# A second group of FFN tiles in plain products, and the first convolution tap on ACT, in a four-layer encoder

## The chip, the cores and the metric

The kernel runs on one core of a Trainium2 chip. The metric is device microseconds of one execution. The engines are PE (TensorE: matmuls; PEld is its weight load), DVE (VectorE), ACT (ScalarE), POOL (GpSimd) and SP (which issues most DMAs).

## The reference

An encoder of four layers over T = 528 tokens (16 meta tokens and 512 of the sequence) with 1024 features. Each layer has a mixer (MLA, RWKV-7, RG-LRU, MLA in turn), a layer norm, a feed-forward part (FFN) and a layer norm. The change lies in the FFN alone:

```python
def _conv_glu_ffn(x, w_in, conv_w, conv_b, w_out):
    g, u = jnp.split(x @ w_in, 2, axis=-1)
    g = _dw_conv(g, conv_w, conv_b, FFN_CONV_LEFT)
    return (jax.nn.silu(g) * u) @ w_out
...
f = _conv_glu_ffn(h, ffn_w_in[i], ffn_conv_w[i], ffn_conv_b[i], ffn_w_out[i])
h = _layer_norm(DN_ALPHA * h + f, ln_g[i, 1], ln_b[i, 1])
```

`w_in` has 1024 x 5632 entries (2816 gate columns and 2816 up columns), the convolution is per channel over 3 tokens, and `w_out` has 2816 x 1024.

## The kernel before, in words

Features lie on partitions, tokens in the free dimension: `h` is eight tiles of 128 x 528. Every matmul operand is split in two fp32r parts, a rounded one (`hi`, a cast on ACT) and the rest (`lo`, a subtraction on DVE or POOL), and a product is three matmuls, hi by hi, lo by hi and hi by lo (`mm3`, L420 to L422), each of 128 x 128 by 264 columns (half of the tokens).

**One FFN** (`ffn`, once per layer) handles the 22 tiles of 128 gate columns and the 22 of up columns in 11 groups. A group is two gate tiles (`kind` 0) and two up tiles (`kind` 1).

- Group 0 is done in plain products, token half by token half: 4 tiles, 8 blocks of features, two halves, three matmuls (L658 to L664). While its first half runs, the layer norm of the second half is still being finished by DVE, ACT and POOL (`late_stats`, `late_apply`, then L554 to L562 in `ln_apply`). ACT copies each finished bank of PSUM into a tile `gp` (L662).
- Groups 1 to 10 go by a Strassen-Winograd scheme (`product`): two tiles by two token halves in seven products of 4 feature blocks, 84 matmuls where plain products take 96. The scheme needs sums of the weights (`products`: four POOL operations L584 to L589, splits L574 and L575) and sums of the operand: `operand_sums` (L606 to L611) makes three new operands (numbers 6, 7 and 4, in `thi`/`tlo`) and writes the fourth (number 5) over a quarter of `xhi`/`xlo` in place. It stands between group 0 and group 1, so that its writes to `xhi`/`xlo` follow group 0's reads. DVE adds each product's bank into its `gp` tile (L638).
- Behind each gate pair come, for each tile, the convolution: a multiply-add with the first tap and the bias on DVE (L694), two more taps on DVE (L697), Silu on ACT (L699). Behind each up pair come the product with the gate (L703, DVE) and the split of the result into `phi`/`plo` (L414 on ACT, L415 on DVE).
- After groups 2, 5 and 8 the finished tiles are multiplied with their part of `w_out` by eight jobs (`partial`), which are taken one per `kind` between the later groups; the rest of `w_out` comes at the end (`residual_out`).

**What sets the order.** The program is written in the order above, and a scheduler of the framework puts each engine's instructions into its own queue by readiness and program order; every engine then works strictly down its queue. Weights come through rings of buffers: `wraw` has 3, `whi` and `wlo` have 4 each, so a weight's cast waits until PE has finished the weight four before it.

Of the kernel before, what the change touches and what calls it, by code (L numbers as in the profile page):

```python
# [8 lines left out]
F32 = mybir.dt.float32  # L9
F32R = mybir.dt.float32r  # L10
I32 = mybir.dt.int32
AF = mybir.ActivationFunctionType
ALU = mybir.AluOpType
# [6 lines left out]
T = META + SEQ  # L20
HT = T // 2
CT = HT // 3
QT = T // 4
KD = D // 128
# [301 lines left out]
class Kern:  # L326
# [265 lines left out]
    def ffn(self, l, split=True):  # L592
        nc, a = self.nc, self.a
        with ExitStack() as es:
            self.banks()
            fp = es.enter_context(self.tc.tile_pool(reuse_waits="tile", name=f"ffn{l}", bufs=1))
# [6 lines left out]
                     5: [q[:, 0, 1] for q in xq], 6: [t[:, 0] for t in ts], 7: [t[:, 1] for t in ts], 4: [t[:, 2] for t in ts]}  # L603
            tmp = [fp.tile([128, K2, HT], F32, name=f"t{i}", tag=n, bufs=6) for i, n in enumerate(("phi", "plo") * 2)]

            def operand_sums():  # L606
                for e, e2, p, out, in0, in1 in SUMS:
                    for c in (slice(0, 2), slice(2, 4)):
                        e.tensor_tensor(out=out[:, c], in0=in0[:, c], in1=in1[:, c], op=ALU.subtract)
                        nc.scalar.copy(pairs[p][0][:, c], out[:, c])  # L610
                        e2.tensor_tensor(out=pairs[p][1][:, c], in0=out[:, c], in1=pairs[p][0][:, c].bitcast(F32), op=ALU.subtract)  # L611

# [45 lines left out]
            for half in range(2):  # L658
                for q in range(4):
                    ps = [self.bank()] * 2  # L660
                    self.lin(ps, [(ws[q], 0, KD)], (self.xhi, self.xlo), [half])
                    nc.scalar.copy(first[q // 2][q % 2][:, 1 + half * HT:1 + half * HT + HT], self.half(ps, half))  # L662
                    if half == 0 and q in (0, 2):
                        self.late_apply() if q else self.late_stats()  # L664
            begin((1, 0))
            operand_sums()
            slots, queue = [], []

            def pieces(m, ch):
                c, n = ch[0], ch[1] - ch[0]  # L670
# [6 lines left out]
            for i in range(KF // 2):  # L677
                cs = []
                for kind in (0, 1):
                    key = (i, kind)  # L680
                    if i:
                        for p in (1, 2, 6, 5, 7, 4, 3):
                            product(key, p)
                        dst = live.pop(key)["t"]
                    else:
                        dst = first[kind]
                    for j in range(2):
                        f = 2 * i + j
                        if kind == 0:
                            gp = dst[j]  # L690
                            nc.gpsimd.memset(gp[:, 0:1], 0.0)
                            nc.gpsimd.memset(gp[:, T + 1:T + 2], 0.0)
                            c = fp.tile([128, T], F32, name="cv", tag="cv", bufs=2)
                            nc.vector.tensor_scalar(out=c, in0=gp[:, 0:T], scalar1=self.p(f"fc_w{l}0", f),  # L694
                                                    scalar2=self.p(f"fc_b{l}", f), op0=ALU.mult, op1=ALU.add)
                            for q in (1, 2):
                                nc.vector.scalar_tensor_tensor(out=c, in0=gp[:, q:q + T], scalar=self.p(f"fc_w{l}{q}", f), in1=c,  # L697
                                                               op0=ALU.mult, op1=ALU.add)
                            nc.scalar.activation(out=c, in_=c, func=AF.Silu)  # L699
                            cs.append(c)  # L700
                        else:
                            c = cs[j]
                            nc.vector.tensor_tensor(out=c, in0=c, in1=dst[j][:, 1:T + 1], op=ALU.mult)  # L703
                            if j == 0:
                                slots.append([fp.tile([128, 2, T], F32R, name=n, tag=n, bufs=6) for n in ("phi", "plo")])
                            self.split(slots[i][0][:, j], slots[i][1][:, j], c)
                    if queue:
                        queue.pop(0)()
# [6 lines left out]
            c = 2 * ch[0]  # L715
# [1201 lines left out]
```

## Time and profile before

| | us |
|---|---|
| three runs | 3535.02, 3537.36, 3537.73 (median 3537.36) |
| the profiled execution's own time | 3529.53 |
| span of that execution in the profile | 3527.7 |
| PE busy / DVE busy / ACT busy / POOL busy in it | 3233.2 / 2806.6 / 1611.0 / 1000.0 |

The profile records one execution. A matmul's record lasts longer than the distance to the next one, since matmuls are pipelined: PE counts as busy as long as one follows on the other. Busy shares are averages over mixers and FFNs, which have different limits; an FFN is read in its own stretch of time. The four FFNs lie at about 420 to 770, 1628 to 1985, 2306 to 2660 and 3124 to 3527 us.

### The profile page before, as it was taken

How to read it: one execution, taken by the hardware profiler on the slowest of the kernel's cores; microseconds unless marked ns; L12 is line 12 of the kernel's file. 1: busy time of each engine (PE TensorE's matmuls, PEld its weight loads, DVE VectorE, ACT ScalarE, POOL GpSimd, SP SyncE). 2: the span in 40 equal slices, each digit the busy share in tenths (PEclk: the TensorE clock that was granted, in tenths of full speed). 3: DMA queues.
4: the chain of work that ended last, by engine and by line, in shares of the span. 5: the costliest groups of instructions: out<-in, count | busy, mean ns of one | idle time of the engine just before them, and what ended most of it. 6: DMA issues, size and time to landing. Idle time of an engine off the chain costs nothing.

```text
span 3527.7 us, 77857 instructions
## 1 busy us (share of the span) xinstructions
PE 3233.2 (92%) x31961; PEld 3105.2 (88%) x31961; DVE 2806.6 (80%) x5166; ACT 1611.0 (46%) x3043; POOL 1000.0 (28%) x1438
## 2 busy tenths in 40 slices
PE   8999989997988988888999988989999899989998
PEld 7899889996977877878899988979999799879998
DVE  6877799979346667658999778799986777789997
ACT  6665443333332333224343478543334666543433
POOL 0000253422015555524533100054331000045341
PEclk9999999998989999989999999999999999999999
DMA  2101213222312112122232212212322011112322
GB/s 82 34 34 41 79 66 106 95 89 88 141 63 46 34 40 47 24 80 68 92 103 93 89 60 73 84 60 89 108 84 81 20 37 34 67 49 90 102 92 71
DMA packets 157717, 250.06 MB, mean 71 GB/s; under 512 B 78736, under 2 KB 88112, under 8 KB 157232
## 3 DMA queue, kind: packets, MB, share of 16 engines
q1 hardware_dynamic: 157360, 245.08, 22.2%
q8 instruction: 251, 4.11, 0.5%
q14 instruction: 106, 0.87, 0.1%
HBM read 227.93 MB, written 17.10 MB: 69 GB/s over the span
## 4 chain that ended last, share of the span: by engine, by line
PE 41%; DVE 16%; ACT 5%; issue 3%; POOL 2%; DMA 1%; SPq 0%; DVEq 0%; ACTq 0%; POOLq 0%
PE bank L422 9%; PE bank L420 9%; PE bank L421 9%; PE pj L218 4%; PE ps L218 3%; DVE wlo L575 2%; PE s L218 1%; PE ch L218 1%; PE rb L218 1%; DVE cv L697 1%; PE yp L218 1%; DVE wlo L409 1%; DVE gp L638 1%; DVE cv L703 1%; DVE cv L694 1%
## 5 line engine op out<-in xcount | busy, mean ns | idle before, releaser
L421 PE MATMUL bank<-xlo,whi 128*128 128x264 f32 x2144 | 621.7, 291 | 22.3 <-DVE xlo L562 11.8
L422 PE MATMUL bank<-xhi,wlo 128*128 128x264 f32 x2144 | 617.2, 291 | 23.6 <-DVE wlo L575 20.4
L420 PE MATMUL bank<-xhi,whi 128*128 128x264 f32 x2144 | 612.3, 291 | 18.2 <-ACT whi L408 13.4
L421 PEld LDWEIGHTS bank<-xlo,whi 128*128 128x128 f32 x2144 | 413.8, 193 | 30.2 <-DVE xlo L562 16.9
L422 PEld LDWEIGHTS bank<-xhi,wlo 128*128 128x128 f32 x2144 | 412.8, 193 | 29.9 <-DVE wlo L575 25.4
L420 PEld LDWEIGHTS bank<-xhi,whi 128*128 128x128 f32 x2144 | 409.9, 193 | 20.9 <-ACT whi L408 13.9
L422 PE MATMUL bank<-phi,wlo 128*128 128x264 f32 x1408 | 402.5, 286 | 2.2 <-DVE wlo L409 2.1
L420 PE MATMUL bank<-phi,whi 128*128 128x264 f32 x1408 | 401.8, 285 | 0.0
L421 PE MATMUL bank<-plo,whi 128*128 128x264 f32 x1408 | 401.4, 285 | 0.0
L574 ACT CAST whi<-wraw 128x1024 fp32r<-128x1024 f32 (+1 forms) x240 | 217.3, 907 | 260.6 <-PE bank L421 166.1
L409 DVE TENSOR_TENSOR wlo<-wraw,whi 128x1024 fp32r<-128x1024 f32 (+1 forms) x218 | 245.2, 1125 | 112.3 <-ACT whi L408 105.4
L575 DVE TENSOR_TENSOR wlo<-wraw,whi 128x1024 fp32r<-128x1024 f32 (+1 forms) x240 | 325.1, 1356 | 8.8 <-ACT whi L574 8.7
L422 PE MATMUL bank<-thi,wlo 128*128 128x264 f32 x960 | 277.8, 290 | 21.4 <-DVE wlo L575 21.4
L408 ACT CAST whi<-wraw 128x1024 fp32r<-128x1024 f32 (+1 forms) x218 | 205.6, 947 | 186.4 <-PE bank L421 142.8
L421 PE MATMUL bank<-tlo,whi 128*128 128x264 f32 x960 | 275.8, 287 | 0.0
L420 PE MATMUL bank<-thi,whi 128*128 128x264 f32 x960 | 274.9, 287 | 0.0
L422 PEld LDWEIGHTS bank<-phi,wlo 128*128 128x128 f32 x1408 | 265.7, 189 | 2.9 <-DVE wlo L409 2.9
L420 PEld LDWEIGHTS bank<-phi,whi 128*128 128x128 f32 x1408 | 266.1, 189 | 0.0
L421 PEld LDWEIGHTS bank<-plo,whi 128*128 128x128 f32 x1408 | 265.7, 189 | 0.0
L589 POOL TENSOR_TENSOR wraw<-wraw,wsum 128x512 f32<-128x512 f32 x80 | 112.3, 1403 | 390.9 <-DVE wlo L575 320.0
L422 PEld LDWEIGHTS bank<-thi,wlo 128*128 128x128 f32 x960 | 183.7, 192 | 24.3 <-DVE wlo L575 24.3
L420 PEld LDWEIGHTS bank<-thi,whi 128*128 128x128 f32 x960 | 183.8, 191 | 0.0
(402 smaller groups left out, 9842.1 us busy)
## 6 DMA issues: line engine op xcount, KB each, us to landing
wraw<-in_ffn_in_dram SPq DMA_DIRECT2D x176, 512.0 KB
wraw<-in_ffn_out_dram SPq DMA_DIRECT2D x96, 384.0 KB
wraw<-in_mla_o_dram SPq DMA_DIRECT2D x48, 256.0 KB
wraw<-in_rw_rkv_dram SPq DMA_DIRECT2D x24, 512.0 KB
wraw<-in_lru_in_dram SPq DMA_DIRECT2D x20, 512.0 KB
wraw<-in_mla_q_dram SPq DMA_DIRECT2D x16, 512.0 KB
wraw<-in_ffn_out_dram SPq DMA_DIRECT2D x16, 512.0 KB
rkv<-ro SPq DMA_DIRECT2D x24, 264.0 KB
```

Source lines behind the costliest of these rows:

```text
L218: op.fn(*op.args, **op.kw)
L408: nc.scalar.copy(hi[:, :cols], raw[:, :cols])
L409: nc.vector.tensor_tensor(out=lo[:, :cols], in0=raw[:, :cols], in1=hi[:, :cols].bitcast(F32), op=ALU.subtract)
L420: nc.tensor.matmul(out, lhsT=w[0][ws], rhs=x[0][xs], start=start, stop=False)
L421: nc.tensor.matmul(out, lhsT=w[0][ws], rhs=x[1][xs], start=False, stop=False)
L422: nc.tensor.matmul(out, lhsT=w[1][ws], rhs=x[0][xs], start=False, stop=stop)
L574: nc.scalar.copy(hi[:, cut], x[:, cut])
L575: nc.vector.tensor_tensor(out=lo[:, cut], in0=x[:, cut], in1=hi[:, cut].bitcast(F32), op=ALU.subtract)
L589: e.tensor_tensor(out=a1[:, 1], in0=a1[:, 1], in1=s[:, 1], op=ALU.subtract)
L638: add = lambda out, x: nc.vector.tensor_tensor(out=out, in0=x, in1=ps, op=ALU.add)
L694: nc.vector.tensor_scalar(out=c, in0=gp[:, 0:T], scalar1=self.p(f"fc_w{l}0", f), scalar2=self.p(f"fc_b{l}", f), op0=ALU.mult, op1=ALU.add)
L697: nc.vector.scalar_tensor_tensor(out=c, in0=gp[:, q:q + T], scalar=self.p(f"fc_w{l}{q}", f), in1=c, op0=ALU.mult, op1=ALU.add)
```

## The change

Group 1 is done in plain products too, by a new function `plain(kind)`: it loads the two tiles' weights one after the other, multiplies both token halves, and ACT copies the four banks into `gp` tiles. `operand_sums` is called twice: behind group 0 it makes all four sums and the splits of operands 6, 7 and 4; behind `plain(1)` it makes the split of operand 5 alone, into `xhi`/`xlo`. The first weights of group 2 are begun there too. In all groups the first tap with its bias moves from DVE to an `Identity` activation on ACT.

```diff
--- before.py
+++ after.py
@@ -603,10 +603,13 @@
                      5: [q[:, 0, 1] for q in xq], 6: [t[:, 0] for t in ts], 7: [t[:, 1] for t in ts], 4: [t[:, 2] for t in ts]}
             tmp = [fp.tile([128, K2, HT], F32, name=f"t{i}", tag=n, bufs=6) for i, n in enumerate(("phi", "plo") * 2)]
 
-            def operand_sums():
+            def operand_sums(splits):
                 for e, e2, p, out, in0, in1 in SUMS:
                     for c in (slice(0, 2), slice(2, 4)):
-                        e.tensor_tensor(out=out[:, c], in0=in0[:, c], in1=in1[:, c], op=ALU.subtract)
+                        if 6 in splits:
+                            e.tensor_tensor(out=out[:, c], in0=in0[:, c], in1=in1[:, c], op=ALU.subtract)
+                        if p not in splits:
+                            continue
                         nc.scalar.copy(pairs[p][0][:, c], out[:, c])
                         e2.tensor_tensor(out=pairs[p][1][:, c], in0=out[:, c], in1=pairs[p][0][:, c].bitcast(F32), op=ALU.subtract)
 
@@ -662,9 +665,22 @@
                     nc.scalar.copy(first[q // 2][q % 2][:, 1 + half * HT:1 + half * HT + HT], self.half(ps, half))
                     if half == 0 and q in (0, 2):
                         self.late_apply() if q else self.late_stats()
-            begin((1, 0))
-            operand_sums()
+            operand_sums((6, 7, 4))
             slots, queue = [], []
+
+            def plain(kind):
+
+                dst = [fp.tile([128, T + 2], F32, name="gp", tag="gp", bufs=4) for j in range(2)]
+                for j in range(2):
+                    w = self.weights(a["ffn_in"][l, 2 + kind, :, j * 1024:j * 1024 + 1024], 1024)
+                    ps = [self.bank(), self.bank()]
+                    self.lin(ps, [(w, 0, KD)], (self.xhi, self.xlo), (0, 1))
+                    for half in range(2):
+                        nc.scalar.copy(dst[j][:, 1 + half * HT:1 + half * HT + HT], self.half(ps, half))
+                if kind:
+                    operand_sums((5,))
+                    begin((2, 0))
+                return dst
 
             def pieces(m, ch):
                 c, n = ch[0], ch[1] - ch[0]
@@ -678,7 +694,9 @@
                 cs = []
                 for kind in (0, 1):
                     key = (i, kind)
-                    if i:
+                    if i == 1:
+                        dst = plain(kind)
+                    elif i:
                         for p in (1, 2, 6, 5, 7, 4, 3):
                             product(key, p)
                         dst = live.pop(key)["t"]
@@ -691,8 +709,7 @@
                             nc.gpsimd.memset(gp[:, 0:1], 0.0)
                             nc.gpsimd.memset(gp[:, T + 1:T + 2], 0.0)
                             c = fp.tile([128, T], F32, name="cv", tag="cv", bufs=2)
-                            nc.vector.tensor_scalar(out=c, in0=gp[:, 0:T], scalar1=self.p(f"fc_w{l}0", f),
-                                                    scalar2=self.p(f"fc_b{l}", f), op0=ALU.mult, op1=ALU.add)
+                            nc.scalar.activation(out=c, in_=gp[:, 0:T], func=AF.Identity, scale=self.p(f"fc_w{l}0", f), bias=self.p(f"fc_b{l}", f))
                             for q in (1, 2):
                                 nc.vector.scalar_tensor_tensor(out=c, in0=gp[:, q:q + T], scalar=self.p(f"fc_w{l}{q}", f), in1=c,
                                                                op0=ALU.mult, op1=ALU.add)
```

**Where the order changes: ACT at the end of group 0, first FFN.** `gp` tiles are the products, `thi` and `xhi` the rounded operand sums, `whi` the rounded weights, `cv` the convolution. Before:

```order
L662 COPY gp_4892<-bank_5097 128x264
L662 COPY gp_4893<-bank_5123 128x264
L574 CAST whi_5203<-wraw_5201 128x1024
L662 COPY gp_4894<-bank_5149 128x264
L610 CAST thi_4886<-t3_4891 128x528
L610 CAST xhi_74<-t0_4888 128x2x264
L610 CAST thi_4886<-t3_4891 128x528
L610 CAST xhi_74<-t0_4888 128x2x264
L574 CAST whi_5290<-wsum_5286 128x1024
```

and now:

```order
L665 COPY gp_4892<-bank_5097 128x264
L665 COPY gp_4893<-bank_5123 128x264
L613 CAST thi_4886<-t3_4891 128x528
L712 ACTIVATE cv_5223<-gp_4892,par_64 128x528
L665 COPY gp_4894<-bank_5149 128x264
L613 CAST thi_4886<-t3_4891 128x528
L712 ACTIVATE cv_5230<-gp_4893,par_64 128x528
L408 CAST whi_5246<-wraw_5245 128x1024
L716 ACT_TABLE_LOAD
L716 ACTIVATE cv_5223<-cv_5223 128x528
```

The first weight of the next group was cast behind two copies; now two taps (L712), a copy and two casts of sums stand ahead of it. The casts into `xhi` are gone from here.

**DVE at the same place** (`t3` is the last operand sum, `wlo` the low part of a weight). Before:

```order
L609 TENSOR_TENSOR t3_4891<-h_68,t1_4889 128x528
L694 TENSOR_SCALAR cv_5237<-gp_4892,par_64 128x528
L575 TENSOR_TENSOR wlo_5204<-wraw_5201,whi_5203 128x1024
L697 SCALAR_TENSOR_TENSOR cv_5237<-gp_4892,par_64,cv_5237 128x528
L611 TENSOR_TENSOR xlo_75<-t0_4888,xhi_74 128x2x264 x2
L697 SCALAR_TENSOR_TENSOR cv_5237<-gp_4892,par_64,cv_5237 128x528
L694 TENSOR_SCALAR cv_5244<-gp_4893,par_64 128x528
```

and now:

```order
L610 TENSOR_TENSOR t3_4891<-h_68,t1_4889 128x528
L714 SCALAR_TENSOR_TENSOR cv_5223<-gp_4892,par_64,cv_5223 128x528 x2
L714 SCALAR_TENSOR_TENSOR cv_5230<-gp_4893,par_64,cv_5230 128x528 x2
L409 TENSOR_TENSOR wlo_5247<-wraw_5245,whi_5246 128x1024
L720 TENSOR_TENSOR cv_5223<-cv_5223,gp_4894 128x528
L720 TENSOR_TENSOR cv_5230<-cv_5230,gp_4895 128x528
```

One tap and the first weight followed the sums; now four tap operations (the two taps of two tiles) come ahead of the first weight, and both subtractions into `xlo` are gone from here.

**ACT in a later group** (the cast of a weight `whi`, the taps and the Silu of `cv`, the copy `pu` of a first product). Before:

```order
L574 CAST whi_5993<-wraw_5991 128x1024
L574 CAST whi_6034<-wsum_6030 128x1024
L574 CAST whi_6067<-wraw2_6029 128x1024
L574 CAST whi_6101<-wraw_5991 128x512
L699 ACTIVATE cv_5933<-cv_5933 128x528
L699 ACTIVATE cv_5940<-cv_5940 128x528
L640 COPY pu_5999<-bank_6001 128x264
```

and now:

```order
L574 CAST whi_5973<-wraw_5971 128x1024
L574 CAST whi_6014<-wsum_6010 128x1024
L574 CAST whi_6047<-wraw2_6009 128x1024
L712 ACTIVATE cv_5913<-gp_5789,par_64 128x528
L712 ACTIVATE cv_5920<-gp_5790,par_64 128x528
L716 ACTIVATE cv_5913<-cv_5913 128x528
L574 CAST whi_6081<-wraw_5971 128x512
L716 ACTIVATE cv_5920<-cv_5920 128x528
L643 COPY pu_5979<-bank_5981 128x264
```

The two taps and one Silu now stand between the casts of the next pair's third and fourth weights.

## Rows read from the trace of the kernel before

**Rows 1.** The page, part 1: busy time, share of the span, instructions.

```profile
PE 3233.2 (92%) x31961; PEld 3105.2 (88%) x31961; DVE 2806.6 (80%) x5166; ACT 1611.0 (46%) x3043; POOL 1000.0 (28%) x1438
```

**Rows 2.** Windows: 60 us behind each layer's first group; then 160 steady us.

```profile
core 0: us, PE busy (x) PEld busy (x) DVE busy (x) ACT busy (x) POOL busy (x), PEclk, DMA share, GB/s
452.00:512.00 60.00, 49.91 (x363) 48.44 (x362) 58.48 (x73) 25.89 (x36) 32.40 (x29) 0.91 0.21 69
1657.00:1717.00 60.00, 48.45 (x368) 46.57 (x367) 58.06 (x73) 26.17 (x37) 33.03 (x30) 0.97 0.21 68
2346.00:2406.00 60.00, 49.28 (x355) 47.70 (x354) 59.08 (x73) 25.74 (x36) 33.39 (x29) 0.91 0.21 69
3155.00:3215.00 60.00, 49.38 (x357) 47.79 (x356) 59.08 (x73) 25.81 (x36) 33.34 (x29) 0.91 0.21 69
560.00:720.00 160.00, 160.00 (x1315) 160.00 (x1314) 145.14 (x202) 63.17 (x84) 60.76 (x60) 1.00 0.31 99
```

**Rows 3.** Timeline of PE, first FFN: start, us; in brackets the idle time before.

```profile
451.96 0.28 PE L421 MATMUL bank<-xlo,whi 128*128 128x264 f32 x1
...
459.26 0.39 PE L422 MATMUL bank<-thi,wlo 128*128 128x264 f32 x1 [3.25 <-DVE wlo L575]
...
477.66 0.59 PE L422 MATMUL bank<-thi,wlo 128*128 128x264 f32 x1 [1.59 <-DVE wlo L575]
...
509.08 0.39 PE L422 MATMUL bank<-xhi,wlo 128*128 128x264 f32 x1 [2.09 <-DVE wlo L575]
```

**Rows 4.** Windows of 5 us, first FFN, columns as in rows 2.

```profile
428.00:433.00 5.00, 5.00 (x44) 5.00 (x44) 3.36 (x17) 1.04 (x3) 0.00 (x0) 1.00 0.62 206
458.00:463.00 5.00, 3.74 (x19) 3.74 (x20) 5.00 (x5) 2.01 (x4) 3.58 (x2) 0.69 0.00 0
478.00:483.00 5.00, 5.00 (x24) 5.00 (x24) 4.08 (x5) 0.71 (x1) 4.92 (x3) 0.50 0.56 197
```

**Rows 5.** Groups by line: xcount, busy us, mean ns of one, idle before.

```profile
L697 DVE SCALAR_TENSOR_TENSOR cv<-gp,par,cv 128x528 f32<-128x528 f32 x176 | 128.0, 780 | 0.0
...
L694 DVE TENSOR_SCALAR cv<-gp,par 128x528 f32<-128x528 f32 x88 | 91.7, 1078 | 0.0
...
L218 ACT ACTIVATE h<-h,par 128x528 f32<-128x528 f32 x8 | 6.6, 821 | 13.1 <-DVE h L218 13.1
```

**Rows 6.** Timeline of DVE, first FFN, around the end of its first group.

```profile
446.97 1.82 DVE L609 TENSOR_TENSOR t<-h,t 128x528 f32<-128x528 f32 x1
...
449.33 0.69 DVE L609 TENSOR_TENSOR t<-h,t 128x528 f32<-128x528 f32 x1
449.95 0.54 DVE L694 TENSOR_SCALAR cv<-gp,par 128x528 f32<-128x528 f32 x1
450.41 2.36 DVE L575 TENSOR_TENSOR wlo<-wraw,whi 128x1024 fp32r<-128x1024 f32 x1
...
453.37 3.54 DVE L611 TENSOR_TENSOR xlo<-t,xhi 128x528 fp32r<-128x528 f32 x2
...
458.00 1.21 DVE L575 TENSOR_TENSOR wlo<-wsum,whi 128x1024 fp32r<-128x1024 f32 x1
...
462.03 1.78 DVE L697 SCALAR_TENSOR_TENSOR cv<-gp,par,cv 128x528 f32<-128x528 f32 x1
```

**Rows 7.** Timeline of ACT, the same place.

```profile
447.65 0.66 ACT L662 COPY gp<-bank 128x264 f32<-128x264 f32 x2 [1.38 <-PE bank L422]
448.19 1.07 ACT L574 CAST whi<-wraw 128x1024 fp32r<-128x1024 f32 x1
449.14 0.40 ACT L662 COPY gp<-bank 128x264 f32<-128x264 f32 x1
449.41 0.66 ACT L610 CAST thi<-t 128x528 fp32r<-128x528 f32 x1
```

**Rows 8.** Timeline of POOL, the same place.

```profile
450.14 1.55 POOL L611 TENSOR_TENSOR tlo<-t,thi 128x528 fp32r<-128x528 f32 x1 [1.92 <-ACT thi L610]
...
461.10 2.14 POOL L585 TENSOR_TENSOR wsum<-wsum,wraw 128x512 f32<-128x512 f32 x1
```

## The prediction

> **What bounds the kernel now.** The page's first part comes first: PE is busy 92% of the span, DVE 80% [rows 1]. That is an average; the change is in four stretches, so I read those. In the steady part of an FFN the window of 160 us shows PE busy all of them at granted clock 1.00, while DVE is busy 145 us, ACT 63 and POOL 61 [rows 2]. There PE alone sets the pace, and its pitch is 160/1315 = 0.1217 us a matmul. The four windows of 60 us behind each layer's first group show the opposite: PE busy 48 to 50 of 60 us, granted clock 0.91 to 0.97, DVE busy 58 to 59 [rows 2]. So PE waits for DVE there, and the gain has to come from these stretches. PE's timeline says on what: the last matmul of group 0 starts at 451.96, then PE waits 3.25 us and 1.59 us for a weight's low part from DVE, and once more 2.09 us at 509 [rows 3]. The clock says what follows: a window of 5 us around the first wait is granted 0.69, and the one behind the second 0.50, which is the lower level, 1.2 GHz, while PE never idles in it [rows 4]. DVE's timeline shows the cause. At 449.95 it does a tap, then a weight's low part in 2.36 us, then two subtractions into `xlo` in 3.54 us [rows 6]: operand sums, weights and taps of two groups meet in one queue.
>
> **What the change adds on PE.** 96 matmuls instead of 84 for two tiles, two kinds, four layers: 12 x 8 = 96 matmuls, at 0.1217 us **+11.7 us**, all on the path.
>
> **What it takes off DVE.** 88 first taps, 91.7 us [rows 5]; in each layer, also 14 of the additions out of PSUM and four of the eight weight splits of group 1; and the operand-5 subtractions go from the crowded place to the end of a group that PE spends 23.4 us on (192 x 0.1217). In the steady part this is worth nothing, since PE does not wait there. ACT gets 88 taps. The nearest row is the `Identity` with a scale and a bias per partition on 128 x 528: 0.82 us [rows 5], so 72 us in all, on an engine busy 63 of 160 us in the steady part. The order shows no further table load ahead of the taps.
>
> **What PE no longer waits for.** Idle time in the four windows: 10.1 + 11.6 + 10.7 + 10.6 = 43.0 us [rows 2]. I take all of it as removed, **-43.0 us**, and price the new wait by itself.
>
> **The new wait, at the start of group 1.** PE is through with group 0 at 452.1 [rows 3]. ACT ends two copies at 448.3 [rows 7]; then come, in the new order: the cast of `t3`'s first half, which DVE has ready at 448.8 [rows 6], at 0.66 to 449.5; a tap, 450.3; a copy, 450.7; a cast, 451.3; the other tap, 452.1; and only then the first weight's cast, 1.07, to 453.2 [rows 7]. PE stands still 1.1 us, does four matmuls that need no low part, and waits again at 453.7. On DVE four tap operations stand ahead of that low part, the last two of them not before 452.1.
> - Low end: at their mean of 0.78 us [rows 5] they end at 453.7, the low part takes 1.2 [rows 6], PE waits 1.2 more: 2.3 us a layer.
> - In between: POOL does two `tlo` subtractions meanwhile, from 449.5 to about 453. Beside POOL a tap took 1.78 us [rows 6, 8], and two `xlo` subtractions 3.54 [rows 6]. If the first two taps are stretched so, they end at 453.8, the others at 455.3, the low part at 456.5: 3.9 us a layer.
> - High end: all four at 1.78 and the low part at the 2.36 of [rows 6]: 459.8, so 7.2 us a layer.
>
> I take 3.9, because the taps do start beside POOL, as the one at 462.03 did: 4 x 3.9 = **+15.6 us**. The Trainium skill bears on this choice: "GPSIMD Engine Reference", section "Specifications", says that POOL shares its SBUF interfaces with DVE and that DVE instructions with two SBUF inputs contend. By that rule the middle or the high end holds; by the mean of 176 taps in [rows 5], which are hardly ever stretched, the low end, a sum lower by 6.4 us. The tap at 462.03 agrees with the rule.
>
> **What hides the rest.** From 456.5 PE needs the second weight at 461.9 (44 matmuls later), then one every 5.8 us. DVE has two multiplies and a split ahead of that time; even at 1.8, 1.8 and 1.2 us it is done at 461.3. That is the thinnest cover, 0.6 us. The transfer of the fourth weight can be issued only when the first weight is split, 456.5; two such transfers fit in 5 us (206 GB/s in [rows 4], 512 KB each), so it is there by about 462, needed at 473.5. Each weight still takes two transfers per pair, so SP's queue gets no longer. The split of operand 5 waits until PE has read its quarter in the last tile, 476.4; two casts at 0.66 and two subtractions at 1.8 end by 481.3; PE wants them as its fourth product of group 2, at 479.4 + 3 x 1.46 = 483.8. Behind ACT's wait for PE there stand the cast of group 2's last weight and the `phi` cast, both needed later.
>
> **The clock.** Busy time by (1 - clock) in the four windows is 49.9 x 0.09 + 48.5 x 0.03 + 49.3 x 0.09 + 49.4 x 0.09 = 14.8 us [rows 2]. Bounds for what stays: nothing, or all of it. With one long wait per layer instead of several I leave one dip, at the mean of the two shown, (3.74 x 0.31 + 5 x 0.5)/2 = 1.8 us [rows 4], 7.3 us in all: **-7.5 us**.
>
> **Sum.** 11.7 - 43.0 + 15.6 - 7.5 = -23.2 us. The profiled execution took 3529.5 us, 1.9 more than its span, so 3506 us by its like; the median of the runs shown stands 7.8 us above it, so on that scale 3537.4 - 23.2 = **3514 us**.
>
> **Rivals.**
> 1. *The group starts almost without a wait.* Taps at their mean, 2.3 us a layer, and PE keeps the clock: 11.7 - 43.0 + 9.2 - 14.8 = -37 us, **3500 us**. For it: the window with the most idle time, 11.6 us, kept the highest clock, 0.97 [rows 2], and 176 taps average 0.78 us. Against it: the first two taps meet POOL.
> 2. *The new wait eats the gain.* At the high end, with the clock dips as now: 11.7 - 43.0 + 28.8 = -2.5 us, **3535 us**, no change. For it: DVE ran a weight's low part in 2.36 us just here [rows 6]. Against it: POOL has nothing to do after 453, because the weight sums of group 2 now need a transfer that starts only when the second weight is split.
> 3. *Slower: ACT becomes the late link.* The place is the end of each gate pair in groups 2 to 10, 36 pairs. There the next pair's third cast, the two taps and the first Silu stand ahead of the fourth cast; before, that cast stood ahead of the Silus. The third cast waits for PE to end the pair (time 0), is done at 1.1; taps on ACT until 2.7; DVE's taps start at 2.4, behind a split, and three of them at 0.78 end at 4.7; the Silu, bounded by a tap's 0.82, ends at 5.6, the cast, bounded by 0.66, at 6.2, its split, bounded by 1.2, at 7.4. PE needs it after a `w_out` job of 36 matmuls (4.4 us) and six products (8.8 us), at 13.1, so there is cover of nearly 6 us, or 1.8 if four taps are stretched by 1.0. (Behind group 2's gate pair no such job lies, and there the order keeps the fourth cast ahead of the taps.) It turns to slower when PE loses over 30/36 = 0.84 us at each; at 1.2 us the time is 3514 + 43 = **3557 us**. The Trainium skill, "ScalarE: Activation LUTs", section "Rules for kernel authors", speaks against this edit: multiply and add belong on VectorE. On a free DVE [rows 6] agrees, 0.54 us against ACT's 0.82; over the kernel the DVE taps average 1.08 [rows 5].
>
> **How the numbers follow.** About 0.2%, 7 us, is what a measurement of this kernel can tell from no change. The forecast (3505 to 3527) gets 0.58, rival 1 0.22, rival 2 0.14, of which 0.04 still falls below 3530, and rival 3 0.06. So faster 0.84, same 0.10, slower 0.06. The range 3498 to 3532 takes in rival 1 and the forecast, with the new wait anywhere between 2.3 and about 6.5 us a layer; the high end of rival 2 and rival 3 are left out.
>
> **What would show it.** Right: 96 more PE matmuls; in the 60 us behind each first group PE idle 4 us instead of 10 or 11, nearly all of it within 5 us of the group's start, on the cast and on the low part of the first plain weight; no wait for DVE near 509 us; steady part still fully busy; DVE tap groups 92 us shorter, ACT's at 0.82 each. Wrong: PE waiting in later groups behind a weight's fourth cast (rival 3); waits of 6 us and more at the start (rival 2); or waits for the second weight, or for operand 5, at the end of group 1, which I costed at nothing.

## The result and the profile after

The changed kernel takes 3481.6 us in the median (3473.3 to 3486.1) against 3537.0: ratio 0.9845, interval 0.9832 to 0.9859. Run again beside the experiments it took 3487.5 against 3534.7: 0.986, interval 0.9834 to 0.9886. So it is 47 to 55 us faster, where 23 were forecast. The profiled execution, the fastest of the four, took 3473.3 us, 56.2 less than the one before.

Busy times on the page, part 1, answering to [rows 1]:

```profile
PE 3216.4 (93%) x32057; PEld 3099.1 (89%) x32057; DVE 2701.7 (78%) x5006; ACT 1673.0 (48%) x3139; POOL 936.7 (27%) x1406
```

There are 96 more matmuls, as worked out. For where the time went I take windows of 115 us from the end of each group 0 on, first of the kernel before, then of the changed one, and last 160 us of its steady part; columns as in [rows 2].

```profile
452.00:567.00 115.00, 103.27 (x793) 100.99 (x792) 112.96 (x143) 47.16 (x65) 56.01 (x52) 0.96 0.25 83
1657.50:1772.50 115.00, 101.87 (x798) 99.18 (x797) 112.54 (x145) 46.95 (x65) 56.94 (x52) 0.99 0.27 85
2346.00:2461.00 115.00, 103.76 (x797) 101.63 (x796) 113.56 (x144) 47.02 (x65) 56.71 (x52) 0.96 0.26 84
3155.00:3270.00 115.00, 103.80 (x797) 101.60 (x796) 113.20 (x144) 47.07 (x65) 56.59 (x52) 0.96 0.26 85
```

```profile
451.50:566.50 115.00, 112.81 (x914) 112.44 (x913) 101.85 (x130) 57.95 (x84) 46.76 (x50) 0.99 0.28 92
1645.50:1760.50 115.00, 112.80 (x926) 112.44 (x924) 104.32 (x133) 58.75 (x85) 47.22 (x50) 1.00 0.30 96
2314.50:2429.50 115.00, 111.57 (x900) 111.13 (x900) 101.96 (x128) 59.19 (x85) 47.78 (x51) 0.99 0.27 88
3110.20:3225.20 115.00, 112.80 (x915) 112.59 (x914) 101.83 (x131) 57.86 (x85) 47.66 (x50) 0.99 0.28 92
...
560.00:720.00 160.00, 160.00 (x1313) 160.00 (x1312) 141.75 (x192) 70.42 (x94) 60.36 (x60) 1.00 0.32 101
```

Count matmuls, not busy time. What PE loses is the window less its matmuls times the pitch of 0.1217 us. Before: 460 - 3185 x 0.1217 = 72.4 us. After: 460 - 3655 x 0.1217 = 15.2 us. That is -57.2, and with +11.7 for the added matmuls -45.5 us. (The counts take in two or three matmuls a window that began before it; counted by their starts alone, the losses are 73.7 and 16.3.) Split up:

| us, four layers | before | after | change | forecast |
|---|---|---|---|---|
| idle (460 - busy) | 47.3 | 10.0 | -37.3 | -43.0 + 15.6 = -27.4 |
| clock (busy x (1 - clock)) | 13.5 | 3.4 | -10.1 | -7.5 |
| in neither (the rest of the loss) | 11.6 | 1.8 | -9.8 | 0 |
| 96 matmuls | | | +11.7 | +11.7 |
| sum | | | -45.5 | -23.2 |

The granted clock stands in the rows with two digits, so its line and the next are each good to about 2 us. The line "in neither" can be read on PE's timeline of the kernel before, around its wait of 3.25 us at 459.26 [rows 3]:

```profile
455.73 0.28 PE L421 MATMUL bank<-tlo,whi 128*128 128x264 f32 x1
...
459.48 0.28 PE L420 MATMUL bank<-thi,whi 128*128 128x264 f32 x1
```

From 455.73 to 459.48 lie two steps, 3.75 us instead of 0.24: 3.51 lost, of which the bracket shows 3.25. The last matmul's record still counts as busy for 0.28 us where the next could have started after 0.12, and the first one behind the wait needs 0.22 until its successor. The windows before hold 36 such waits; 11.6 / 36 is about 0.3 us each.

The waits that are left stand at the start of group 1. PE's timeline of the changed kernel, first and third FFN:

```profile
451.69 0.28 PE L421 MATMUL bank<-xlo,whi 128*128 128x264 f32 x1
454.17 0.51 PE L422 MATMUL bank<-xhi,wlo 128*128 128x264 f32 x2 [2.19 <-DVE wlo L409]
...
2315.29 0.39 PE L420 MATMUL bank<-xhi,whi 128*128 128x264 f32 x1 [0.70 <-ACT whi L408]
2318.77 0.59 PE L422 MATMUL bank<-xhi,wlo 128*128 128x264 f32 x2 [2.73 <-DVE wlo L409]
```

The second and the fourth FFN are like the first. DVE's timeline in the first, then POOL's, then DVE's first and third tap in windows of one tap each:

```profile
448.18 4.80 DVE L714 SCALAR_TENSOR_TENSOR cv<-gp,par,cv 128x528 f32<-128x528 f32 x4 [0.19 <-ACT cv L712]
452.90 1.22 DVE L409 TENSOR_TENSOR wlo<-wraw,whi 128x1024 fp32r<-128x1024 f32 x1
```

```profile
447.50 1.68 POOL L614 TENSOR_TENSOR tlo<-t,thi 128x528 fp32r<-128x528 f32 x1 [1.31 <-ACT thi L613]
449.52 1.41 POOL L614 TENSOR_TENSOR tlo<-t,thi 128x528 fp32r<-128x528 f32 x1 [0.34 <-ACT thi L613]
```

```profile
448.18 1.55 DVE L714 SCALAR_TENSOR_TENSOR cv<-gp,par,cv 128x528 f32<-128x528 f32 x1 [0.19 <-ACT cv L712]
...
451.42 0.76 DVE L714 SCALAR_TENSOR_TENSOR cv<-gp,par,cv 128x528 f32<-128x528 f32 x1
```

Four taps take 4.80 us: 1.55 and 1.73 for the two beside POOL's `tlo`, 0.76 and 0.77 for the two behind it. The first low part stands behind them. That PE waits 2.2 us in one layer and 3.4 in another comes from the clock just before, in group 0's second half (first and third FFN):

```profile
433.60:451.20 17.60, 14.55 (x97) 13.36 (x96) 16.77 (x21) 11.76 (x24) 14.14 (x11) 0.90 0.00 1
2298.20:2314.30 16.10, 13.13 (x97) 11.93 (x96) 15.29 (x20) 10.53 (x23) 13.25 (x11) 1.00 0.01 1
```

At a clock of 0.90 PE needs 17.6 us for this half instead of 16.1. It comes to group 1 later by 1.5 us and so waits less, for DVE's low part begins 19.3 us behind the start of this half in either layer. Half and stretch behind it together come out alike, 118.1 us in either layer. In the run again two layers had the lower clock there and waited 2.2 us, the other two had not and waited 3.4; in the kernel before no layer had it.

Groups by line, ACT's tap and then DVE's other two taps:

```profile
L712 ACT ACTIVATE cv<-gp,par 128x528 f32<-128x528 f32 x88 | 69.1, 824 | 37.7 <-DVE gp L641 36.7
```

```profile
L714 DVE SCALAR_TENSOR_TENSOR cv<-gp,par,cv 128x528 f32<-128x528 f32 x176 | 177.7, 1059 | 10.8 <-ACT cv L712 9.9
```

DVE's first taps (91.7 us [rows 5]) are gone, but its other two went from 780 to 1059 ns, 49.7 us in all.

Outside these stretches the profiled executions differ by another 10.7 us (56.2 - 45.5), and a part of that is the change too. Group 0 has the same matmuls in both kernels, but its first part, from its first matmul to the middle, takes 70.9 us in four layers instead of 79.5, in both profiles of the changed kernel alike. Third FFN, PE before, then POOL before, then PE and POOL of the changed kernel:

```profile
2319.68 0.39 PE L421 MATMUL bank<-xlo,whi 128*128 128x264 f32 x1 [1.94 <-POOL xlo L562]
```

```profile
2315.17 1.35 POOL L585 TENSOR_TENSOR wsum<-wsum,wraw 128x512 f32<-128x512 f32 x1
2316.47 1.47 POOL L587 TENSOR_TENSOR wraw<-wraw,wraw 128x512 f32<-128x512 f32 x1
2317.90 1.72 POOL L562 TENSOR_TENSOR xlo<-h,xhi 128x264 fp32r<-128x264 f32 x1
```

```profile
2289.81 0.39 PE L421 MATMUL bank<-xlo,whi 128*128 128x264 f32 x1 [1.15 <-POOL xlo L562]
```

```profile
2288.17 1.58 POOL L562 TENSOR_TENSOR xlo<-h,xhi 128x264 fp32r<-128x264 f32 x1 [1.67 <-ACT xhi L561]
```

Before, the sums of group 1's weights (L585, L587) stood on POOL ahead of an `xlo` that PE waited for. With group 1 in plain products there are no such sums. The first and the fourth FFN are like the third; in the second, two waits of 0.9 and 0.8 us are gone. Group 0's second half, on the other hand, took 4.5 us more than before (3.0 in the run again), by the clock shown above. So group 0 as a whole is shorter by 4.0 us, in the run again by 5.6.

The rest is 6.5 us shorter than before in the first profile and 11.6 us longer in the one run again. 750 us of the second layer's mixer in these two profiles:

```profile
840.00:1590.00 750.00, 664.67 (x11889) 609.05 (x11888) 448.44 (x1073) 244.75 (x541) 282.09 (x695) 0.94 0.22 60
```

```profile
850.00:1600.00 750.00, 663.58 (x11812) 610.50 (x11812) 438.88 (x1060) 241.34 (x535) 280.07 (x692) 0.92 0.22 59
```

The same kernel, 0.94 and 0.92 of the clock. From the end of the first layer's stretch to the second layer's group 0 the one took 1059 us and the other 1073; the kernel before took 1059. This is the spread of such stretches from one execution to the next and no effect of the change. Group 0 and the stretches behind it give -49.7 and -48.2 us, between the 47 and 55 us of the medians.

### The profile page after: what moved, and what is told of

Its sections match the earlier page's. It is cut to its first block, busy times and chain, and to the rows that moved or that the text cites. A ratio compares the mean times of both kernels' runs of the same rounds, so it can differ in the third digit from the quotient of the medians.

```text
span 3471.5 us, 77910 instructions
## 1 busy us (share of the span) xinstructions
PE 3216.4 (93%) x32057; PEld 3099.1 (89%) x32057; DVE 2701.7 (78%) x5006; ACT 1673.0 (48%) x3139; POOL 936.7 (27%) x1406
## 4 chain that ended last, share of the span: by engine, by line
PE 47%; DVE 10%; ACT 6%; issue 2%; POOL 2%; DMA 2%; SPq 0%; DVEq 0%; ACTq 0%; POOLq 0%
PE bank L422 11%; PE bank L421 11%; PE bank L420 11%; PE pj L218 4%; PE ps L218 2%; PE s L218 1%; PE ch L218 1%; PE rb L218 1%; PE yp L218 1%; PE mm L420 1%; PE mm L421 1%; PE mm L422 1%; POOL dt L218 1%; ACT wv L218 1%; ACT th L1227 1%
## 5 line engine op out<-in xcount | busy, mean ns | idle before, releaser
L421 PE MATMUL bank<-xlo,whi 128*128 128x264 f32 x2272 | 655.7, 290 | 18.7 <-DVE xlo L562 10.9
L422 PE MATMUL bank<-xhi,wlo 128*128 128x264 f32 x2272 | 651.2, 289 | 12.4 <-DVE wlo L409 12.3
L420 PE MATMUL bank<-xhi,whi 128*128 128x264 f32 x2272 | 646.6, 289 | 15.4 <-ACT whi L408 13.8
L421 PEld LDWEIGHTS bank<-xlo,whi 128*128 128x128 f32 x2272 | 437.0, 192 | 26.1 <-DVE xlo L562 14.8
L420 PEld LDWEIGHTS bank<-xhi,whi 128*128 128x128 f32 x2272 | 432.7, 192 | 17.5 <-ACT whi L408 14.6
L422 PEld LDWEIGHTS bank<-xhi,wlo 128*128 128x128 f32 x2272 | 435.3, 192 | 14.4 <-DVE wlo L409 14.4
L574 ACT CAST whi<-wraw 128x1024 fp32r<-128x1024 f32 (+1 forms) x216 | 195.2, 904 | 124.2 <-PE bank L421 72.4
L422 PE MATMUL bank<-thi,wlo 128*128 128x264 f32 x864 | 246.3, 285 | 0.0
L421 PE MATMUL bank<-tlo,whi 128*128 128x264 f32 x864 | 245.7, 284 | 0.0
L420 PE MATMUL bank<-thi,whi 128*128 128x264 f32 x864 | 244.9, 283 | 0.0
L714 DVE SCALAR_TENSOR_TENSOR cv<-gp,par,cv 128x528 f32<-128x528 f32 x176 | 177.7, 1059 | 10.8 <-ACT cv L712 9.9
```

Source lines behind the costliest of these rows:

```text
L420: nc.tensor.matmul(out, lhsT=w[0][ws], rhs=x[0][xs], start=start, stop=False)
L421: nc.tensor.matmul(out, lhsT=w[0][ws], rhs=x[1][xs], start=False, stop=False)
L422: nc.tensor.matmul(out, lhsT=w[1][ws], rhs=x[0][xs], start=False, stop=stop)
L574: nc.scalar.copy(hi[:, cut], x[:, cut])
```

## The experiments

All runs in one table. "Stretches" is the time from the start of group 0's last matmul to the same place of the work some 600 matmuls behind group 1, the four layers added, in the profiled execution; it keeps the mixers' spread out. With PE at its pitch it would be 793 x 4 x 0.1217 = 386.0 us for one plain group. The last column begins at group 0's first matmul instead. It is the better one for differences of a few us, because in it a lower clock in group 0's second half and the shorter wait behind it cancel. Group 0's first part took 79.5 us in the two kernels with group 1 in seven products, and 70.9 or 71.0 in all the others.

| kernel | median us | ratio to before, interval | stretches us | with group 0 |
|---|---|---|---|---|
| before | 3535 to 3541 in five comparisons | | 448.0 | 592.4 |
| changed, and again | 3481.6, 3487.5 | 0.9845, 0.986 | 402.4, 405.5 | 542.7, 544.2 |
| plain group only | 3493.8 | 0.9875 (0.9846 to 0.9903) | 416.4 | 552.3 |
| tap only | 3532.5 | 0.9994 (0.9979 to 1.0009) | 441.5 | 589.0 |
| first weight ahead, and again | 3472.0, 3475.7 | 0.9815 (0.9789 to 0.984), 0.9825 (0.9809 to 0.984) | 391.9, 392.9 | 532.3, 531.8 |
| two plain groups | 3498.5 | 0.9897 (0.9878 to 0.9916) | 415.5 | 554.3 |
| tap on ACT in groups 0, 1 alone | 3487.9 | 0.9866 (0.9847 to 0.9884) | 408.8 | 547.6 |
| first weight ahead, taps on DVE | 3486.1 | 0.9861 (0.9842 to 0.9879) | 407.9 | 546.8 |
| first weight ahead, half a plain group | 3483.2 | 0.9853 (0.9827 to 0.9878) | 404.3 | 545.5 |
| all sums late | 3486.0 | 0.9856 (0.984 to 0.9871) | 422.9 | 545.0 |
| one split twice | 3485.9 | 0.9847 (0.9825 to 0.9869) | 407.5 | 546.2 |
| the same, first weight ahead | 3471.1 | 0.9812 (0.9796 to 0.9829) | 391.3 | 528.5 |
| sums behind the gate pair | 3485.7 | 0.9847 (0.9833 to 0.9862) | 423.2 | 545.2 |
| first weight ahead, sums on POOL | 3471.1 | 0.9805 (0.9789 to 0.9822) | 389.9 | 531.8 |

**The changed kernel again.**

> The changed kernel again, for the spread of its own runs and as the one to compare the others with on this chip: ratio 0.983 to 0.986 to the kernel before. If the half-rate stretches outside the FFNs are luck of a run, they differ between this run and the first one by several us, with the same instructions there.

0.986, as expected, and the mixers differed, as shown above.

**The plain group alone.**

```diff
-nc.scalar.activation(out=c, in_=gp[:, 0:T], func=AF.Identity, ...)
+nc.vector.tensor_scalar(out=c, in0=gp[:, 0:T], ..., op0=ALU.mult, op1=ALU.add)
```

> The second group in plain products as in the change, but the first tap with its bias stays on DVE in all groups. Theory (the gain comes from the 90 us behind each group 0, where DVE is late): in the FFN stages DVE has one or two more taps ahead of the first plain weight's low part, 0.54 to 1.8 us each, so PE's wait at the start of group 1 goes from 2.2 to 3.3 to 5.8 us a layer; all else as in the changed kernel, the steady part fully busy. That is 4 to 14 us above the changed kernel (3481.6): 3486 to 3496 us, ratio to the kernel before 0.985 to 0.988. Rival (the tap move makes the gain): the gain of 55 us mostly goes, over 3510 us, ratio above 0.992.

The median fell into the theory's range, in part by luck, as PE's waits show. DVE's timeline at the first group 1, then PE's:

```profile
449.63 3.04 DVE L712 TENSOR_SCALAR cv<-gp,par 128x528 f32<-128x528 f32 x2
452.59 2.80 DVE L715 SCALAR_TENSOR_TENSOR cv<-gp,par,cv 128x528 f32<-128x528 f32 x4
455.31 2.35 DVE L409 TENSOR_TENSOR wlo<-wraw,whi 128x1024 fp32r<-128x1024 f32 x2
```

```profile
456.58 0.81 PE L422 MATMUL bank<-xhi,wlo 128*128 128x264 f32 x2 [2.99 <-DVE wlo L409]
...
512.95 0.39 PE L422 MATMUL bank<-phi,wlo 128*128 128x264 f32 x1 [0.63 <-DVE wlo L409]
```

Six taps stand ahead of the low part in 5.8 us, and PE waits 3.0 us for it in every layer, 3.2 with a short wait for the cast. The theory had 3.3 to 5.8; the changed kernel waits 3.4 where its clock stays full, as it did here in all four layers. So the start is not what got longer. What got longer are later waits that the theory left out, one of 0.3 to 1.0 us and one of 0.5 in each layer. The plain group alone brings 31.6 us in the stretches, its own 11.7 paid, and 40.1 with group 0.

**The tap alone**, in the kernel before:

```diff
-nc.vector.tensor_scalar(out=c, in0=gp[:, 0:T], ..., op0=ALU.mult, op1=ALU.add)
+nc.scalar.activation(out=c, in_=gp[:, 0:T], func=AF.Identity, ...)
```

> The kernel before with only the first tap and its bias moved to ACT in all groups; group 1 stays in seven products. Theory: behind group 0 DVE sheds the taps of groups 0 and 1, four of about 1 us a layer, of the 18 to 19 us that PE lost there a layer; the operand sums, weight splits and additions stay crowded, so PE's idle time in the four windows of 60 us goes from 43 to 28 to 38 us, and the time from 3537 to 3520 to 3532 us, ratio 0.995 to 0.9985. Rival (the tap move makes the gain): 3500 us or less, ratio under 0.99. Second rival (ACT is the late link when its queue gets longer): 3537 us or more.

Less than the theory's range: no difference in the median, 6.5 us in the stretches, 3.4 with group 0. PE's timeline, then DVE's:

```profile
458.69 0.28 PE L421 MATMUL bank<-xlo,whi 128*128 128x264 f32 x1
462.63 0.39 PE L422 MATMUL bank<-thi,wlo 128*128 128x264 f32 x1 [3.66 <-DVE wlo L575]
```

```profile
454.65 3.57 DVE L611 TENSOR_TENSOR xlo<-t,xhi 128x528 fp32r<-128x528 f32 x2
458.14 3.30 DVE L696 SCALAR_TENSOR_TENSOR cv<-gp,par,cv 128x528 f32<-128x528 f32 x3
461.36 1.22 DVE L575 TENSOR_TENSOR wlo<-wsum,whi 128x1024 fp32r<-128x1024 f32 x1
```

Taking taps off DVE does not help while the split of operand 5 (3.57 us) and the other taps still stand ahead of the low part that PE needs next. With group 0, the two parts together bring 48.2 to 49.7 us, alone 40.1 + 3.4 = 43.5.

**The first weight of group 1 ahead of the sums.**

```diff
+w1 = self.weights(a["ffn_in"][l, 2, :, 0:1024], 1024)
 operand_sums((6, 7, 4))
...
-w = self.weights(...)
+w = self.weights(...) if kind or j else w1
```

> The changed kernel with the first plain weight of group 1 loaded and split ahead of the operand sums and taps in program order (its low part then stands ahead of the four taps on DVE). Theory (the wait at group 1's start is the taps' alone): the waits of 2.2 to 3.4 us at the start of group 1 go, with the 0.2 us of pitch that each costs beside its idle time, and the dips of the clock behind them: 9 to 14 us below the changed kernel, 3468 to 3473 us, ratio to the kernel before 0.980 to 0.982. Rival (the wait moves on: taps and products now stand ahead of the second or third weight's low part, or of the split of operand 5): PE waits at the second or third weight by about as much, 3478 to 3484 us.

> The version with the first weight of group 1 ahead, again, as the base of the run before and for its own spread: ratio 0.980 to 0.983 to the kernel before.

15.5 us below the changed kernel on the same chip in the median, rather more than expected, and 10.4 to 12.4 us with group 0, within the theory's 9 to 14. This beats both kernels. DVE's timeline of the second run:

```profile
449.74 1.21 DVE L409 TENSOR_TENSOR wlo<-wraw,whi 128x1024 fp32r<-128x1024 f32 x1
451.25 4.58 DVE L715 SCALAR_TENSOR_TENSOR cv<-gp,par,cv 128x528 f32<-128x528 f32 x4 [0.30 <-ACT cv L713]
```

The low part is done at 451, the taps, nearly as slow as before, behind it. A window of the first run, in the first layer, shows what PE loses then: 115 - 935 x 0.1217 = 1.2 us.

```profile
452.50:567.50 115.00, 114.36 (x935) 113.76 (x935) 108.21 (x135) 58.88 (x86) 51.02 (x52) 1.00 0.30 95
```

**Two plain groups** (`plain(i, kind)` for groups 1 and 2, the split of operand 5 behind group 2).

> The changed kernel with group 2 in plain products as well, the split of operand 5 and the first weights of group 3 behind it. Theory (after group 1 nothing is left to gain, PE is the bound there): 12 more matmuls a pair, 96 in all, at 0.1217 us, 11.7 us, less at most the 2.2 us that the changed kernel still loses in the 600 matmuls behind group 1: 9 to 12 us above the changed kernel, ratio to the kernel before 0.988 to 0.990 where the changed kernel stood at 0.986. Rival (DVE is still behind at the end of group 1, and a second plain group gives it more air): equal to the changed kernel or below it, 0.986 or less.

10.1 to 11.6 us more with group 0, 0.9897 against 0.986: the price of 96 matmuls, and DVE has nothing left to catch up that would be worth it.

**The ACT tap in groups 0 and 1 alone.**

```diff
+if i < 2:
     nc.scalar.activation(out=c, in_=gp[:, 0:T], func=AF.Identity, ...)
+else:
+    nc.vector.tensor_scalar(out=c, in0=gp[:, 0:T], ..., op0=ALU.mult, op1=ALU.add)
```

> The changed kernel with the first tap on ACT in groups 0 and 1 alone; in groups 2 to 10 it is back on DVE. Theory (the later taps are hidden behind PE): as the changed kernel within 4 us, ratio 0.985 to 0.987. Rival (in the steady part too a tap ahead of a weight's low part costs something): 72 taps a kernel, over 10 us slower, 0.989 or more.

The theory holds: no difference that the medians can tell, 3.4 to 4.9 us with group 0, where PE now waits once for 0.5 us in each layer.

**The first weight ahead, but the taps on DVE.**

> The first weight of group 1 split ahead of sums and taps, as in the faster version, but the first tap on DVE in all groups. Theory (the tap move is worth only what it takes from ahead of the first plain weight's low part): with that weight first, the tap move is worth 0 to 8 us (the taps now stand ahead of the second weight's), I take 3: 3472 to 3480 us, ratio 0.9815 to 0.984. Rival (the tap move is worth its 13 us in the FFN stages whatever the order): 3485 us, 0.985 or more.

The rival holds: 14.5 to 15.0 us more with group 0 than the version with the first weight ahead. PE's timeline:

```profile
497.53 0.39 PE L422 MATMUL bank<-xhi,wlo 128*128 128x264 f32 x1 [1.62 <-DVE wlo L575]
...
509.37 0.39 PE L422 MATMUL bank<-phi,wlo 128*128 128x264 f32 x1 [1.07 <-DVE wlo L409]
```

These longest waits lie in and behind group 2, not at group 1, where two of the layers wait 0.6 us: DVE comes level later, and then the later taps count too. In the run with the start wait kept and the taps of groups 0 and 1 on ACT, the same later taps cost one wait of 0.5 us.

**Half a plain group** (only `kind` 0 of group 1 plain, the split of operand 5 and `begin((1, 1))` behind it).

> The version with the first weight ahead, but only the gate pair of group 1 in plain products; its up pair goes by seven products again, with the split of operand 5 behind the gate pair. It saves 12 matmuls a layer, 5.8 us. Theory (one plain pair of 23.4 us is needed for DVE to come level): DVE has 11.7 us less cover a layer, its backlog meets the weight sums of the up pair and the split of operand 5, and PE waits 1.5 us or more a layer: no gain, 3472 to 3484 us, ratio 0.9815 to 0.985. Rival (half a group is cover enough): 5.8 us less than the version with the first weight ahead, 3466 us, 0.980.

The theory holds: the medians lie 8 to 11 us above those with the whole group, although there are 48 matmuls fewer. PE's timeline:

```profile
485.50 0.39 PE L422 MATMUL bank<-xhi,wlo 128*128 128x264 f32 x1 [0.55 <-DVE wlo L575]
...
497.80 0.39 PE L422 MATMUL bank<-xhi,wlo 128*128 128x264 f32 x1 [1.79 <-DVE wlo L575]
```

**All sums late, and sums behind the gate pair.**

```diff
-operand_sums((6, 7, 4))
...
-operand_sums((5,))
+operand_sums((5, 6, 7, 4))
```

> The changed kernel with all operand sums (not the split of operand 5 alone) called behind group 1. Theory (what counts is which DVE work stands ahead of a weight's low part): with the sums away from the start of group 1 the first weight is split ahead of the taps, and the wait there goes; the sums then stand on DVE in the middle of group 1, where PE's 23.4 us a pair cover them: 3472 to 3484 us, ratio to the kernel before 0.9815 to 0.985, that is below the changed kernel's 0.986. Rival (that the sums are made while group 1 begins is a part of the gain): PE waits for thi or tlo at the third product of group 2, over 1 us a layer on top: 3490 us or more.

> The changed kernel with the sums and the splits of operands 6, 7 and 4 called behind the gate pair of group 1 instead of behind group 0; the split of operand 5 stays behind the up pair, as in the change. In the run with all sums late, group 0's second half was 4.4 us a layer shorter and group 2 began with waits for xhi (3.1 us) and xlo (1.6 us). Theory (those waits came from the split of operand 5 being called together with the other sums): they go, group 0 keeps its gain, and the time is 4 x 4.5 = 18 us below that run: 3464 to 3472 us, ratio to the kernel before 0.9795 to 0.982. Rival (they come from DVE and POOL having the sums in the middle of group 1, whatever the call): as the run with all sums late, 3480 to 3488 us, 0.984 to 0.9865.

The first fell between theory and rival, and its waits are on `xhi` and `xlo`, which neither had named; the second is the rival's. Both equal the changed kernel in the median, because two effects cancel: the stretches are 17 to 21 us longer, and group 0's second half is 4 to 5 us a layer shorter. The longest of PE's waits in it, in the version with the first weight ahead (second run), then with all sums late, and there those of group 2 too:

```profile
443.12 0.39 PE L421 MATMUL bank<-xlo,whi 128*128 128x264 f32 x1 [0.33 <-POOL xlo L562]
...
446.89 0.39 PE L421 MATMUL bank<-xlo,whi 128*128 128x264 f32 x1 [1.92 <-DVE xlo L562]
```

```profile
440.82 0.39 PE L421 MATMUL bank<-xlo,whi 128*128 128x264 f32 x1 [0.15 <-POOL xlo L562]
...
478.30 0.39 PE L420 MATMUL bank<-xhi,whi 128*128 128x264 f32 x1 [3.05 <-ACT xhi L613]
...
480.27 0.59 PE L421 MATMUL bank<-xlo,whi 128*128 128x264 f32 x1 [1.58 <-DVE xlo L614]
```

The last two rows are the other effect: with the sums in the middle of group 1 the split of operand 5 is late for group 2, whether it is in the same call or not. So the place of the sums is worth nothing by itself: behind group 0 they hold up its last low parts, inside group 1 the split of operand 5.

**The split of operand 7 twice**, behind group 0, in both versions.

```diff
+for _ in range(2 if p == 7 else 1):
     nc.scalar.copy(pairs[p][0][:, c], out[:, c])
     e2.tensor_tensor(out=pairs[p][1][:, c], in0=out[:, c], in1=..., op=ALU.subtract)
```

> The changed kernel with the split of operand 7 done twice behind group 0: two more casts on ACT (0.66 us) and two more subtractions on DVE (0.7 to 1.8 us) a layer, the same work as the split of operand 5 that the change moved behind group 1. Theory (every us on DVE ahead of the first low part is a us of PE): the wait at the start of group 1 grows by 1.4 to 3.6 us a layer: 6 to 14 us above the changed kernel, ratio 0.9875 to 0.990. Rival (hidden by the wait for the taps or the cast): as the changed kernel, 0.986.

> The same doubled split of operand 7, but in the version with the first weight ahead of the sums and taps. Theory (the price of DVE work there depends on its place in the queue): the first weight is no longer behind it, so most is hidden; one of the subtractions stands ahead of the first low part's successor only: 0 to 4 us above the version with the first weight ahead, ratio 0.9815 to 0.983. Rival (DVE has no room left in group 1, all its work there is on the path): 6 to 14 us more, as in the run before, 0.9835 to 0.986.

In the changed kernel the rival holds: it costs 2.0 to 3.5 us with group 0 and nothing in the median. The timelines of DVE, POOL and PE show why:

```profile
453.15 2.79 DVE L715 SCALAR_TENSOR_TENSOR cv<-gp,par,cv 128x528 f32<-128x528 f32 x4
455.87 2.34 DVE L409 TENSOR_TENSOR wlo<-wraw,whi 128x1024 fp32r<-128x1024 f32 x2
```

```profile
449.32 3.34 POOL L615 TENSOR_TENSOR tlo<-t,thi 128x528 fp32r<-128x528 f32 x2 [1.39 <-ACT thi L614]
```

```profile
454.86 0.39 PE L420 MATMUL bank<-xhi,whi 128*128 128x264 f32 x1 [1.62 <-ACT whi L408]
```

The taps come later, when POOL is through with `tlo`, and all four take 2.79 us instead of 4.80, which gives back 2.0 us. The first low part is still 1.2 us later behind group 0 than in the changed kernel. PE now waits 1.6 us here for ACT's cast of the first weight, does eight matmuls that need no low part, with 0.2 us between them, and then waits 0.6 us for DVE. With the first weight ahead the doubled split is free.

**Sums of DVE on POOL** (in `SUMS` operands 6 and 4 from `(v, g, ...)` to `(g, v, ...)`, first weight ahead).

> The version with the first weight ahead, with the two sums that DVE makes (for operands 6 and 4) on POOL and their tlo subtractions on DVE instead; the work on DVE is as long as before, but DVE waits for POOL and ACT in its place. Theory (group 0's second half waits 1.9 us for the last xlo because sums stand ahead of it on DVE): the subtractions that stand ahead of it now are as many, so nothing changes in group 0, 3470 to 3480 us, ratio 0.981 to 0.984. Rival (POOL, at 1.3 to 2.0 us a sum, is late, and the casts of thi that wait for it hold up ACT's cast of the first weight): over 3484 us, 0.985 or more.

As the theory said: 531.8 us with group 0, as in the version without. Which of the two engines makes the sums is of no account.

## Why the direction was right and the size was not

- **The stage was right, but too narrow.** Most of the gain came out of the stretches behind group 0, the steady part is still fully busy, and the plain group carries most of it. Group 0 itself, where the prediction expected nothing, gave 8.6 us in its first part.
- **The 96 matmuls** were right; the second plain group measured the price again.
- **The failed step is "What PE no longer waits for", with the clock beside it: 43.0 + 14.8 = 57.8 us as all that PE lost before.** Behind group 0 it was 72.4. Idle time was read in 60 us, but DVE is late for longer: the next 55 us hold 4.3 us more idle time (47.3 against 43.0). And idle plus clock leaves out about 0.3 us at each of 36 waits. The rows for it were there: 60 us with 363 matmuls [rows 2] lost 60 - 363 x 0.1217 = 15.8 us, and the four rows 64.4 in all. The 8.6 us in group 0 are missing from the step as well: the sums of group 1's weights were not sought ahead of group 1.
- **The new wait and the clock that stays** were priced at 15.6 + 7.3 = 22.9 us, which was nearly right: 15.2 behind group 0, and 4.5 more by the clock in its second half, 19.7. The taps came out as the middle case took them, 1.55, 1.73, 0.76 and 0.77 us against 1.78 twice and 0.78 twice, and where the clock stayed full PE waited 3.4 us a layer against 3.9. That three layers show 2.2, as at the low end, is luck of the clock: PE lost 1.5 us ahead of the window instead. The Trainium skill's rule in "GPSIMD Engine Reference", section "Specifications", that DVE instructions with two SBUF inputs contend with POOL, agrees with this trace: 1.55 to 1.73 us beside POOL, 0.76 without. The row at 451.96, read as group 0's last, is already group 1's second matmul; the wait of 0.59 us behind it is in the sum of idle time, so nothing changes by it.
- **The sum closes.** 23.2 forecast, 14.6 more lost before (72.4 against 57.8), 8.6 in group 0's first part, 3.2 less that stays (19.7 against 22.9): 49.6 us, against 49.7 measured from group 0 on.
- **What I costed at nothing** at the end of group 1 stayed at nothing: no wait for the second weight or for operand 5, no lasting loss from the taps on ACT (0.824 us each against my 0.82). The move is worth 8 to 10 us with group 0 beside a plain group (6 us between the medians of one comparison), though nothing measurable alone. The rule of the Trainium skill in "ScalarE: Activation LUTs", section "Rules for kernel authors", would leave multiply and add on VectorE; beside a plain group this case goes the other way.
- **DVE's relief** from the taps was less than half of what I said, 42.0 of 91.7 us: its other taps grew by 49.7 us. In the trace 58 of these 176 lie for the most part beside an operation of POOL and take 1.67 us in the mean, and the other 118 take 0.76; before, 12 lay so and 164 took 0.76. It comes from the move to ACT, since with the plain group alone 14 lie so, with the tap alone 68. Nothing waited for it.
- **The rivals.** The first, a start with little wait, was nearest and still 12 to 18 us too slow, since it rested on the same 57.8 us. The second and third did not show.

Left open: why the clock falls in group 0's second half in some layers and executions and not in others, with the same instructions there.

## What to carry to other kernels

Price what an engine loses as window less count times pitch, not as idle time by busy share: a busy share hides a part of each wait, and a window cut where the trouble looks over, or begun where the change begins in the program, hides the rest: instructions of the next group had been queued into this one. When one queue feeds the bound engine, its order matters more than its load: splitting the first weight ahead of four taps was worth 10 to 12 us, and doubling other work behind it cost nothing. And take a gain from the stage where it arises, since identical stages of two executions differed by 13 us here.

## What I had not expected of the hardware

- A stall of PE costs more than its recorded idle time, 0.26 us more in the wait shown and about 0.3 in the mean of 36.
- The same mixer's instructions ran at a granted clock of 0.94 and 0.92 in two executions of one kernel, 1059 and 1073 us from the first layer's stretch to the second layer's group 0.
- A lower clock just ahead of a wait can cost nothing: PE came to group 1 1.5 us later and waited 1.2 us less.
- Work that starts later can take less time: with two more subtractions ahead, four taps took 2.79 us instead of 4.80, because POOL had finished meanwhile. The low part behind them still came 1.2 us later.
